# Scaling token tiles before a plain transpose and folding the pre-norm weights into the rounding, in the opening of a hybrid attention block on one core

## The chip, the cores and the metric

The kernel runs on one core of one Trainium2 chip. The metric is the device time of that core in microseconds (us). Engines are named as the profile names them: PE is the matrix engine (its weight loads are listed as PEld), DVE the vector engine, ACT the scalar engine, POOL the general-purpose engine; SP only issues transfers here.

## The reference

One decoder layer on x of 512 tokens by 1024 channels, in float32. Only its first lines bear on the change:

```python
def rms_norm(x, g):
    xf = x.astype(jnp.float32)
    y = xf * lax.rsqrt(jnp.mean(xf * xf, axis=-1, keepdims=True) + RMS_EPS)
    return (y * g.astype(jnp.float32)).astype(x.dtype)

def hybrid_layer(x, norm_pre, w_in, pe_k, w1_k, w2_k, pe_v, w1_v, w2_v, w_a, w_b, w_o, norm_post):
    u = rms_norm(x, norm_pre)
    proj = u @ w_in            # 1024 x 5912: q, k, v, gates, z of two branches, merge gates
    ...                        # compressed, selected and window attention; block attention; gated output projection
    return x + rms_norm(m @ w_o, norm_post)
```

## The kernel before

**What the opening makes.** Every later projection needs u transposed, channels on partitions, and split in two parts: `uh` (u rounded to fp32r) and `ul` (the rest, u − uh), each 128 partitions x 8 channel groups x 512 tokens. A product with a weight split in the same way into hi and lo is three matmuls: hi x uh, hi x ul, lo x uh. The 512 tokens come as four tiles (`tt` = 0 to 3) of 128 tokens x 1024 channels. Per tile the opening computes sums of squares (ACT, `x_stats`), the mean plus epsilon (a small DVE instruction), the power −1/2 on POOL (the result is `rs`), and then transposes in two halves (`h`), four 128x128 transposes each, into a PSUM tile `ut`.

**Tiles 0 and 1 and tiles 2 and 3 differ.** For tiles 0 and 1 (`x_diag`) DVE builds diag(rs), and PE multiplies the x tile with it, which transposes and scales in one matmul (L588). For tiles 2 and 3 ACT first scales x by rs (`x_scale`, L579) and PE then transposes against the identity (L590). In both cases `x_hi` follows for each half: one DVE multiply by the pre-norm weights `npreT` (128x512, L596), one ACT rounding to `uh` (128x512, L600), and `x_low` subtracts on DVE or POOL (128x512, L604).

**The first product, `a_mm`.** For each token tile, 24 matmuls (L626; parts 0, 1, 2 are hi x uh, hi x ul, lo x uh, 8 channel groups each) of 128 tokens by 280 columns of `w_in` go into one PSUM tile `pa`. These 280 columns (`ra`) arrive in four transfers and are split by `wa_hi` (ACT or POOL) and `wa_lo` (DVE or POOL), two channel groups at a time. PSUM tiles `pa` have the tag "s", which has two buffers: tile 2 takes the buffer of tile 0, and tile 3 that of tile 1. `a_evac_act(tt)` (L636, L637) and `a_evac_dve(tt)` (L642) read `pa` out; the DVE part is the last reader.

**What sets the order.** The opening stands in `with tc.manual_schedule()`: each engine runs its own instructions in the order in which the calls are written there, and waits for another engine only where data or a buffer demand it. After it the long stream of projections begins with `mm_kcvc` (L171, L172, L173, 512 tokens at a time), whose weights are split by the pieces `first[0]` to `first[6]`. Thirteen matmuls on zeros (`keep_warm`) run on PE while x is on its way. The transfers are issued on SP: two halves of tile 0, `npre` (the pre-norm weights), tile 1, `ra`, tiles 2 and 3. `klos` and `rowsel` are tiles of a later stage that POOL fills with constants.

Of the kernel before, what the change touches and what calls it, by code (L numbers as in the profile page):

```python
# [41 lines left out]
def hybrid_block(ctx, tc, x, norm_pre, w_in, pe_k, w1_k, w2_k, pe_v, w1_v, w2_v,  # L42
# [509 lines left out]
    rs, up, sss = {}, {}, {}  # L552

    def x_stats(tt, parts=1):
        sq = s4.tile([128, D], F32, tag="s4", name=f"sq_{tt}")
# [5 lines left out]
        sss[tt] = ss  # L561
        if parts == 2:
            r = rs[tt]
            dve.tensor_scalar(ss[:, 0:1], ss[:, 0:1], 1.0 / D, EPS, op0=ALU.mult, op1=ALU.add)
            dve.scalar_tensor_tensor(r, ss[:, 1:2], 1.0 / D, ss[:, 0:1], op0=ALU.mult, op1=ALU.add)
            pool.tensor_tensor(r, r, neghalf, op=ALU.pow)

    def x_stats_r(tt):
        rstd_of(sss[tt][:, 0:1], rs[tt], EPS)

    diag = {}

    def x_diag(tt):
        diag[tt] = early.tile([128, 128], F32, name=f"diag_{tt}")
        dve.tensor_scalar(diag[tt], ident, rs[tt], None, op0=ALU.mult)

    def x_scale(tt, h):
# [74 lines left out]
    with tc.manual_schedule():  # L652
        keep_warm(13)
        x_stats(0, 2)
        pt = ps("t", "npreT_ps")
# [2 lines left out]
        x_diag(0)
        x_transpose(0, 0)
        x_stats_r(1)  # L660
        dve.tensor_copy(npreT, pt[:, 0:KT])
# [480 lines left out]
```

## Time and profile before

| what | value |
|---|---|
| time, median of 3 runs | 471.25 us (471.22 to 471.26) |
| profiled execution, its own time | 471.45 us |
| its span in the profile | 469.7 us, so 1.75 us lie around it |
| PE busy | 459.0 us, 98% of the span |
| DVE, ACT, POOL busy | 326.4, 255.8, 125.8 us |
| first `mm_kcvc` matmul | 26.97 us from the start of the span |

All starts are in us from the start of the span. A row with "x8" is a group of eight instructions that follow one another; the time beside it is from the first one's start to the last one's end. Instructions of one engine overlap, so the distance from start to start is shorter than a duration.

### The profile page before, as it was taken

To read this page: it belongs to the slowest core of one execution; us is meant where nothing else is said; L and a number is where in the kernel's file an instruction comes from. 1 tells how busy PE (TensorE), PEld (TensorE's weight loads), DVE (VectorE), ACT (ScalarE), POOL (GpSimd) and SP (SyncE) were. 2 spreads that over 40 slices of the span, in tenths; PEclk is the share of its full clock that TensorE was granted. 3 is DMA by queue.
4 is the path that set the end of the run, shared out by engine and by line. 5 is a ranking of instruction groups with operands and counts; after the bars stand their busy time and mean duration, and the time that the engine had idled before them with its cause. 6 is when DMAs were issued, how large, how long until landed. Compare 5 with 4: busy or idle time off the path is not lost.

```text
span 469.7 us, 6991 instructions
## 1 busy us (share of the span) xinstructions
PE 459.0 (98%) x2408; PEld 388.1 (83%) x2408; DVE 326.4 (69%) x837; ACT 255.8 (54%) x684; POOL 125.8 (27%) x144
## 2 busy tenths in 40 slices
PE   7999999999999999999999999999999999999994
PEld 6988887888999888788888888887888888888884
DVE  3858868998777878877798978777674264265044
ACT  5754657776566758656675866675433333234021
POOL 6600006433231333323144443432221010020000
...
GB/s 275 191 161 199 45 51 174 2 77 104 7 84 91 1 91 46 45 89 15 77 91 14 76 89 54 38 92 71 64 93 138 109 63 137 89 89 135 45 134 136
DMA packets 45091, 42.08 MB, mean 90 GB/s; under 512 B 1624, under 2 KB 39808, under 8 KB 45056
## 3 DMA queue, kind: packets, MB, share of 16 engines
...
q10 hardware_dynamic: 144, 0.52, 0.3%
...
q14 instruction: 16, 0.13, 0.1%
...
## 4 chain that ended last, share of the span: by engine, by line
PE 88%; DVE 6%; ACT 3%; POOL 1%; issue 1%; POOLq 0%; DVEq 0%; ACTq 0%
PE t L976 5%; PE mm_ga L171 3%; PE mm_ga L172 3%; PE mm_ga L173 3%; PE mm_gb L172 3%; PE mm_gb L173 3%; PE mm_gb L171 3%; PE s L937 3%; PE s L938 3%; PE o L997 3%; PE o L996 3%; PE pa L626 2%; PE mm_qkb L172 2%; PE mm_qkb L173 2%; PE mm_qkb L171 2%; PE mm_vb L290 2%
## 5 line engine op out<-in xcount | busy, mean ns | idle before, releaser
L943 ACT ACTIVATE p<-p,st 128x512 f32<-128x512 f32 (+3 forms) x96 | 53.1, 555 | 23.5 <-DVE st L941 23.2
L955 POOL TENSOR_SCALAR p<-p,st 128x256 f32<-128x256 f32 (+1 forms) x48 | 44.1, 929 | 64.6 <-DVE st L952 22.9
L977 ACT ACTIVATE pt<-t 128x512 fp32r<-128x512 f32 (+1 forms) x72 | 35.4, 524 | 27.4 <-PE t L976 26.8
L978 DVE TENSOR_TENSOR pt<-t,pt 128x512 fp32r<-128x512 f32 (+1 forms) x72 | 40.8, 594 | 8.1 <-ACT pt L977 7.7
L941 DVE CUSTOM_DVE_ANT_0 p<-s,bias_a 128x512 f32<-128x512 f32 (+3 forms) x64 | 29.1, 484 | 10.5 <-PE s L938 10.4
L976 PE MATMUL t<-ident,p 128*128 128x128 f32 x240 | 34.7, 274 | 1.3 <-DVE pt L978 1.0
L976 PEld LDWEIGHTS t<-ident,p 128*128 128x128 f32 x240 | 27.5, 140 | 6.1 <-DVE pt L978 3.3
L354 POOL TENSOR_TENSOR ga<-ga,gb 128x512 f32<-128x512 f32 x8 | 11.7, 1464 | 77.2 <-DVE gb L353 77.2
L1004 POOL TENSOR_TENSOR z<-ot,z 64x512 f32<-64x512 f32 x16 | 20.6, 1285 | 21.8 <-DVE ot L1003 21.8
L171 PE MATMUL mm_qkb<-uh,ws_qkb 128*128 128x512 f32 x64 | 25.8, 404 | 0.0
L171 PE MATMUL mm_gb<-uh,ws_gb 128*128 128x512 f32 x64 | 25.6, 400 | 0.0
L171 PE MATMUL mm_ga<-uh,ws_ga 128*128 128x512 f32 x64 | 25.6, 400 | 0.0
L955 DVE TENSOR_SCALAR p<-p,st 128x512 f32<-128x512 f32 (+1 forms) x48 | 25.2, 564 | 0.5
L172 PE MATMUL mm_gb<-ul,ws_gb 128*128 128x512 f32 x64 | 25.4, 396 | 0.0
L173 PE MATMUL mm_gb<-uh,ws_gb 128*128 128x512 f32 x64 | 25.3, 396 | 0.0
L172 PE MATMUL mm_qkb<-ul,ws_qkb 128*128 128x512 f32 x64 | 25.3, 395 | 0.0
L172 PE MATMUL mm_ga<-ul,ws_ga 128*128 128x512 f32 x64 | 25.3, 395 | 0.0
L173 PE MATMUL mm_ga<-uh,ws_ga 128*128 128x512 f32 x64 | 25.3, 395 | 0.0
L173 PE MATMUL mm_qkb<-uh,ws_qkb 128*128 128x512 f32 x64 | 25.2, 394 | 0.0
L119 DVE TENSOR_TENSOR ws_ab<-raw_ab,ws_ab 128x256 fp32r<-128x256 f32 x32 | 12.8, 455 | 16.7 <-ACT ws_ab L118 16.7
L895 POOL TENSOR_SCALAR bias_a<-dbase 128x512 f32<-128x512 f32 x8 | 13.2, 1650 | 37.8 <-DVE st L941 33.0
L895 POOL TENSOR_SCALAR bias_b<-dbase 128x512 f32<-128x512 f32 x8 | 12.3, 1543 | 38.2 <-DVE st L941 38.2
...
## 6 DMA issues: line engine op xcount, KB each, us to landing
...
```

Of the source, the lines that this page charges most:

```text
L171: mm(dst, v[:, 0, k], rh(n), start=(n == 0), stop=False)
L172: mm(dst, v[:, 0, k], rl(n), start=False, stop=False)
L173: mm(dst, v[:, 1, k], rh(n), start=False, stop=(n == len(kts) - 1))
L895: pool.tensor_scalar(t, dbase, slope, None, op0=ALU.mult)
L937: mm(sp[:, 0:nn], q, hi, start=True, stop=False)
L941: dve.tensor_tensor_reduce(pp, src, bias[:, 384 - 128 * i:512], 1.0, 3.0e38, ALU.add, ALU.min, st[:, 0, i:i + 1])
L943: act.activation(pp, pp, AF.Exp, bias=st[:, 0, i:i + 1], scale=-1.0, accum_out=st[:, 1, i:i + 1])
L955: (dve if i >= 2 else pool).tensor_scalar(pp, pp, st[:, 1, i:i + 1], None, op0=ALU.mult)
L976: pe_eng.transpose(tp[:, b * 128:(b + 1) * 128], p_of(u, i)[:, 128 * j:128 * j + 128], ident)
L977: act.activation(h[:, c0:c0 + n], tp[:, 0:n], AF.Copy)
L978: dve.tensor_tensor(l[:, c0:c0 + n], tp[:, 0:n], f(h[:, c0:c0 + n]), op=ALU.subtract)
L1004: pool.tensor_tensor(zs[zt][mine], t[mine], zs[zt][mine], op=ALU.mult)
```

## The change

In its parts:

1. `npre` is fetched as the first transfer on ACT's queue, no longer on SP between tiles 0 and 1, and its transpose `npreT` is made earlier, with the last two of the thirteen warm-up matmuls behind it.
2. The constant fills of `klos` and `rowsel`, which POOL ran before its first power, move into `clear()`, called after `first[6]`.
3. All four tiles are scaled on DVE (`x_scale`, one `tensor_scalar` of 128x512 per half) and then transposed against the identity. `diag` and ACT's scaling are gone.
4. The multiply by `npreT` is gone as an instruction. `x_hi` is four ACT instructions of 128x128 per half, which read PSUM and scale by a column of `npreT` while they round; `x_low` is four DVE instructions of 128x128 per half, (ut x npreT) − uh. All `x_low` stand on DVE now, and POOL's share of `wa_lo` too; POOL takes two of the four `wa_hi`.
5. The opening has a new order, with `a_mm` in smaller pieces (channel groups 0 to 3 and 4 to 7 apart).

```diff
+    npre = early.tile([KT, 128], F32, name="npre")
+    nc.scalar.dma_start(npre, norm_pre.rearrange("(k p) -> k p", k=KT))
...
     load_x(0, 2)
-    nc.sync.dma_start(npre, norm_pre.rearrange("(k p) -> k p", k=KT))
     load_x(1)
...
+    def x_scale(tt, h, eng=None):
         c = slice(512 * h, 512 * h + 512)
-        act.activation(xt[tt][:, c], xt[tt][:, c], AF.Copy, scale=rs[tt])
+        if eng is None:
+            dve.tensor_scalar(xt[tt][:, c], xt[tt][:, c], rs[tt], None, op0=ALU.mult)
...
     def x_transpose(tt, h):
-
         pt = ps("to"[h], f"ut_{tt}_{h}")
         for k in range(4):
             kk = 4 * h + k
-            o, i = pt[:, k * 128:(k + 1) * 128], xt[tt][:, kk * 128:(kk + 1) * 128]
-            if tt in diag:
-                mm(o, i, diag[tt], start=True, stop=True)
-            else:
-                pe_eng.transpose(o, i, ident)
-        up[tt, h] = pt
+            pe_eng.transpose(pt[:, k * 128:(k + 1) * 128], xt[tt][:, kk * 128:(kk + 1) * 128], ident)
+        ut[tt, h] = pt
 
     def x_hi(tt, h):
-
-        u = xt[tt][:, 512 * h:512 * h + 512].rearrange("p (k t) -> p k t", k=4)
-        dve.tensor_tensor(u, up[tt, h].rearrange("p (k t) -> p k t", k=4),
-                          npreT[:, 4 * h:4 * h + 4, None].to_broadcast([128, 4, 128]), op=ALU.mult)
-        hi = uh[:, 4 * h:4 * h + 4, tt * 128:tt * 128 + 128]
-        up[tt, h] = (u, hi)
-        act.activation(hi, u, AF.Copy)
-
-    def x_low(tt, h, eng=dve):
-        u, hi = up[tt, h]
-        eng.tensor_tensor(ul[:, 4 * h:4 * h + 4, tt * 128:tt * 128 + 128], u, f(hi), op=ALU.subtract)
+        for k in range(4):
+            kk = 4 * h + k
+            act.activation(uh[:, kk, tt * 128:tt * 128 + 128], ut[tt, h][:, k * 128:(k + 1) * 128], AF.Copy,
+                           scale=npreT[:, kk:kk + 1])
+
+    def x_low(tt, h):
+        for k in range(4):
+            kk = 4 * h + k
+            a = slice(tt * 128, tt * 128 + 128)
+            dve.scalar_tensor_tensor(ul[:, kk, a], ut[tt, h][:, k * 128:(k + 1) * 128], npreT[:, kk:kk + 1],
+                                     f(uh[:, kk, a]), op0=ALU.mult, op1=ALU.subtract)
...
         x_low(2, 0)
+        a_evac_act(0)
+        x_scale(3, 0)
+        a_mm(2, (0,), 2, lo)
+        x_scale(3, 1)
+        x_low(2, 1)
+        a_mm(2, (0,), 2, hi)
+        a_evac_act(1)
+        x_transpose(3, 0)
         x_transpose(3, 1)
         a_evac_dve(0)
-        a_mm(1, (1,), 1)
+        a_mm(2, (2,), 1)
...
-        a_mm(3, (0, 1, 2))
+        a_mm(3, (0, 2, 1), 1)
         first[6]()
+        clear()
```

What stands where is told by each engine's own order. First DVE, from the statistics of tile 2 on (`rs_196`, now `rs_239`) to the read-out of `pa` of tile 0 (L642, now L638, which writes `v_slc` and `v_win`), before:

```order
13 L514 TENSOR_SCALAR rs_196<-ss_195 128x1
14 L613 TENSOR_TENSOR wa_hl<-ra,wa_hl 128x560 x2
15 L514 TENSOR_SCALAR rs_226<-ss_225 128x1
16 L613 TENSOR_TENSOR wa_hl<-ra,wa_hl 128x560
17 L604 TENSOR_TENSOR ul<-x_96,uh 128x4x128
18 L596 TENSOR_TENSOR x_97<-ut_0_250,npreT 128x512
19 L596 TENSOR_TENSOR x_97<-ut_1_264,npreT 128x512
20 L604 TENSOR_TENSOR ul<-x_97,uh 128x4x128
21 L642 TENSOR_TENSOR v_slc<-pa_198,v_slc 128x2x64
22 L642 TENSOR_TENSOR v_win<-pa_198,v_win 128x2x64
```

and now (`x_98`, `x_99`, `x_100` are the token tiles 1, 2, 3; `ut_0_184` and `ut_1_190` belong to tile 1, `ut_0_273` and `ut_1_278` to tile 2):

```order
11 L561 TENSOR_SCALAR rs_239<-ss_238 128x1
12 L589 SCALAR_TENSOR_TENSOR ul<-ut_0_184,npreT,uh 128x128 x4
13 L589 SCALAR_TENSOR_TENSOR ul<-ut_1_190,npreT,uh 128x128 x4
14 L567 TENSOR_SCALAR x_99<-x_99,rs_239 128x512 x2
15 L561 TENSOR_SCALAR rs_285<-ss_284 128x1
16 L599 TENSOR_TENSOR wa_hl<-ra,wa_hl 128x560 x2
17 L589 SCALAR_TENSOR_TENSOR ul<-ut_0_273,npreT,uh 128x128 x4
18 L567 TENSOR_SCALAR x_100<-x_100,rs_285 128x512 x2
19 L589 SCALAR_TENSOR_TENSOR ul<-ut_1_278,npreT,uh 128x128 x4
20 L638 TENSOR_TENSOR v_slc<-pa_199,v_slc 128x2x64
21 L638 TENSOR_TENSOR v_win<-pa_199,v_win 128x2x64
```

Between the statistics of tile 2 and the read-out of tile 0 DVE had seven large instructions and one small; now it has 6 of 128x512 or 128x560, 16 of 128x128 and one small, with the scaling of tile 3 and all of tile 2's `x_low` ahead of the read-out. The second place is ACT, from the first rounding on, before (L610 is `wa_hi`, L600 `x_hi`):

```order
5 L610 ACTIVATE wa_hl<-ra 128x560 x2
6 L600 ACTIVATE uh<-x_95 128x4x128
7 L610 ACTIVATE wa_hl<-ra 128x560
8 L600 ACTIVATE uh<-x_95 128x4x128
9 L560 ACTIVATE sq_194,ss_195<-x_97 128x1024
10 L600 ACTIVATE uh<-x_96 128x4x128 x2
11 L560 ACTIVATE sq_224,ss_225<-x_98 128x1024
12 L579 ACTIVATE x_97<-x_97,rs_196 128x512 x2
13 L579 ACTIVATE x_98<-x_98,rs_226 128x512 x2
```

and now (L582 is `x_hi`, L596 `wa_hi`, L556 the squares of tiles 2 and 3):

```order
6 L582 ACTIVATE uh<-ut_0_156,npreT 128x128 x4
7 L582 ACTIVATE uh<-ut_1_162,npreT 128x128 x4
8 L596 ACTIVATE wa_hl<-ra 128x560
9 L582 ACTIVATE uh<-ut_0_184,npreT 128x128 x4
10 L582 ACTIVATE uh<-ut_1_190,npreT 128x128 x4
11 L596 ACTIVATE wa_hl<-ra 128x560
12 L556 ACTIVATE sq_237,ss_238<-x_99 128x1024
13 L556 ACTIVATE sq_283,ss_284<-x_100 128x1024
```

The squares of tile 2 stood behind three `wa_hi` and two roundings, and stand now behind two `wa_hi` and sixteen small roundings. The third place is PE, around the first product of tile 2 (`pa_311`, now `pa_316`), before (`x_97` and `x_98` are tiles 2 and 3 there, `pa_228` is tile 1):

```order
12 L590 MATMUL ut_0_250<-ident,x_97 128x128 x4
13 L626 MATMUL pa_198<-wa_hl,uh 128x280 x4
14 L590 MATMUL ut_1_264<-ident,x_97 128x128 x4
15 L626 MATMUL pa_228<-wa_hl,uh 128x280 x4
16 L590 MATMUL ut_1_279<-ident,x_98 128x128 x4
17 L590 MATMUL ut_0_288<-ident,x_98 128x128 x4
18 L626 MATMUL pa_228<-wa_hl,ul 128x280 x8
19 L626 MATMUL pa_311<-wa_hl,uh 128x280 x16
20 L626 MATMUL pa_311<-wa_hl,ul 128x280 x8
```

and now (`pa_199`, `pa_221`, `pa_316`, `pa_398` are the products of tiles 0 to 3):

```order
17 L575 MATMUL ut_0_273<-ident,x_99 128x128 x4
18 L575 MATMUL ut_1_278<-ident,x_99 128x128 x4
19 L622 MATMUL pa_199<-wa_hl,uh 128x280 x4
20 L622 MATMUL pa_221<-wa_hl,uh 128x280 x4
21 L622 MATMUL pa_316<-wa_hl,uh 128x280 x8
22 L575 MATMUL ut_0_334<-ident,x_100 128x128 x4
23 L575 MATMUL ut_1_339<-ident,x_100 128x128 x4
24 L622 MATMUL pa_316<-wa_hl,uh 128x280 x8
25 L622 MATMUL pa_316<-wa_hl,ul 128x280 x8
26 L753 MATMUL ps_pe_k<-ident,cv_k 128x16
27 L171 MATMUL mm_kcvc_470<-uh,ws_kcvc_380 128x512
28 L753 MATMUL ps_pe_v<-ident,cv_v 128x16
```

The transposes of tile 3 stood ahead of the first matmul into `pa` of tile 2, with a whole part of tile 1 between them and it; now eight matmuls into `pa` of tile 2 stand ahead of them. The product of tile 3, 24 matmuls, stands now behind the first two matmuls of `mm_kcvc` (L171, L172) and ahead of the third (L173). Behind that L173 the order of every engine is the one of before but for names.

## Rows read from the trace of the kernel before

**Rows 1.** The page: the span, and the engines' busy time, share of the span and instructions.

```profile
span 469.7 us, 6991 instructions
PE 459.0 (98%) x2408; PEld 388.1 (83%) x2408; DVE 326.4 (69%) x837; ACT 255.8 (54%) x684; POOL 125.8 (27%) x144
```

**Rows 2.** Windows of the opening: stretch and its length, busy us (and instructions) of each engine, granted PE clock, share of the DMA engines, GB/s.

```profile
5.00:10.00 5.00, 4.13 (x31) 3.55 (x30) 2.06 (x7) 2.29 (x4) 2.32 (x5) 1.00 1.06 321
10.00:15.00 5.00, 4.17 (x31) 3.56 (x29) 4.80 (x8) 4.19 (x9) 2.99 (x3) 1.00 1.06 368
15.00:20.00 5.00, 5.00 (x41) 4.94 (x42) 4.23 (x9) 4.93 (x11) 3.52 (x6) 1.00 0.89 220
20.00:25.00 5.00, 5.00 (x41) 5.00 (x41) 3.90 (x11) 3.14 (x13) 1.99 (x4) 1.00 0.00 0
```

**Rows 3.** The chain of work that ended last, its opening in order of time: start us, us, what.

```profile
5.82 0.52 POOL klos L752
6.34 0.53 POOL rs L566
6.89 0.30 DVE diag L575
7.24 2.96 PE ut L588 x24
10.22 0.69 DVE x L596
10.91 2.74 DVE ul L604 x2
13.69 3.09 PE pa L626 x20
...
19.61 7.21 PE pa L626 x56
27.04 0.43 PE mm_kcvc L171
```

**Rows 4.** Timeline of the statistics of tiles 0 and 1: start us, us, engine, line, operation, out and in, count, and in brackets the idle time before it and its releaser.

```profile
4.85 0.16 DVE L565 SCALAR_TENSOR_TENSOR rs<-ss 128x1 f32<-128x1 f32 x1 [0.49 <-ACT sq L560]
6.46 1.06 ACT L560 ACTIVATE sq<-x 128x1024 f32<-128x1024 f32 x1 [1.64 <-DMA x<-in_x_dram]
7.42 0.19 ACT L560 ACTIVATION_READ_ACCUMULATOR sq<-x 128x1 f32 x1
7.88 0.55 POOL L515 TENSOR_TENSOR rs<-rs,neghalf 128x1 f32<-128x1 f32 x1 [1.02 <-DVE npreT L661]
14.38 0.98 POOL L515 TENSOR_TENSOR rs<-rs,neghalf 128x1 f32<-128x1 f32 x1 [1.29 <-DVE rs L514]
```

**Rows 5.** Timeline of PE, the same columns: transposes against diag, plain transposes, the first product, and the first rows of `mm_kcvc`.

```profile
7.24 3.84 PE L588 MATMUL ut<-diag,x 128*128 128x128 f32 x32 [0.87 <-DVE diag L575]
18.58 1.03 PE L590 MATMUL ut<-ident,x 128*128 128x128 f32 x8
20.48 2.22 PE L626 MATMUL pa<-wa_hl,uh 128*128 128x280 f32 x16
26.75 0.23 PE L758 MATMUL ps_pe_k<-ident,cv_k 16*128 16x16 f32 x1
26.97 0.51 PE L171 MATMUL mm_kcvc<-uh,ws_kcvc 128*128 128x512 f32 x1
27.32 0.40 PE L172 MATMUL mm_kcvc<-ul,ws_kcvc 128*128 128x512 f32 x1
27.55 0.39 PE L173 MATMUL mm_kcvc<-uh,ws_kcvc 128*128 128x512 f32 x1
```

**Rows 6.** ACT: timeline rows of L579 (128x512 from SBUF, scaled by a column), L600 (128x512 from SBUF, no column) and L636 (128x128 from PSUM, no column), and by source line the one place with 128x128 from PSUM scaled by a column (L811; durations min/median/max in ns).

```profile
15.85 2.73 ACT L579 ACTIVATE x<-x,rs 128x512 f32<-128x512 f32 x4
20.92 1.17 ACT L600 ACTIVATE uh<-x 128x512 fp32r<-128x512 f32 x2 [0.89 <-DVE x L596]
19.01 0.25 ACT L636 ACTIVATE v_slc<-pa 128x128 fp32r<-128x128 f32 x1
19.16 0.26 ACT L636 ACTIVATE v_win<-pa 128x128 fp32r<-128x128 f32 x1
L811 ACT ACTIVATE vcs<-pk_v,rowsel x2: 367/367/367, 82.2 to 83.4; 128x128 fp32r<-128x128 f32 x2
```

**Rows 7.** DVE: timeline rows of L642 (128x128, PSUM and SBUF), of L613 (`wa_lo`) and L596 (128x512), by source line the one place with a 128x128 product with a column and a second operand (L812), and the group of 128x512 products with a column (L955: count, busy us, mean ns).

```profile
19.74 0.28 DVE L642 TENSOR_TENSOR v_slc<-pa,v_slc 128x128 fp32r<-128x128 f32 x1
19.94 0.28 DVE L642 TENSOR_TENSOR v_win<-pa,v_win 128x128 fp32r<-128x128 f32 x1
14.22 1.38 DVE L613 TENSOR_TENSOR wa_hl<-ra,wa_hl 128x560 fp32r<-128x560 f32 x2
20.14 1.28 DVE L596 TENSOR_TENSOR x<-ut,npreT 128x512 f32<-128x512 f32 x2
L812 DVE SCALAR_TENSOR_TENSOR vcs<-pk_v,rowsel,vcs x2: 341/343/345, 83.1 to 84.3; 128x128 fp32r<-128x128 f32 x2
L955 DVE TENSOR_SCALAR p<-p,st 128x512 f32<-128x512 f32 x24 | 12.7, 529 | 0.5
```

**Rows 8.** Windows at the end of the span, columns as in rows 2, and from the timeline of PE the warm-up matmuls (as a whole, and two pieces of it).

```profile
463.00:465.00 2.00, 0.61 (x6) 0.41 (x4) 0.49 (x2) 0.47 (x2) 0.48 (x1) 1.00 0.19 72
465.00:465.50 0.50, 0.00 (x0) 0.00 (x0) 0.40 (x1) 0.00 (x0) 0.07 (x1) 1.00 0.00 0
465.50:466.00 0.50, 0.00 (x0) 0.00 (x0) 0.50 (x2) 0.00 (x0) 0.00 (x0) 0.54 0.00 0
...
1.44 4.78 PE L650 MATMUL warmup<-warmup 128*128 128x512 f32 x13 [1.44 <-DVE warmup L83]
2.03 1.05 PE L650 MATMUL warmup<-warmup 128*128 128x512 f32 x2
4.90 0.62 PE L650 MATMUL warmup<-warmup 128*128 128x512 f32 x2
```

More of the change, by code (lines that the diff above doesn't have):

```diff
@@ L560, in x_stats @@
             act.activation(sq[:, n * w:n * w + w], xt[tt][:, n * w:n * w + w], AF.Square, accum_out=ss[:, n:n + 1])
-        sss[tt] = ss
+        part = EPS
         if parts == 2:
[L563 to L577, printed above, removed]
+            part = ss[:, 0:1]
+            dve.tensor_scalar(part, part, 1.0 / D, EPS, op0=ALU.mult, op1=ALU.add)
+        dve.tensor_scalar(r, ss[:, parts - 1:parts], 1.0 / D, part, op0=ALU.mult, op1=ALU.add)
+        pool.tensor_tensor(r, r, neghalf, op=ALU.pow)
+    def x_scale(tt, h, eng=None):
         c = slice(512 * h, 512 * h + 512)
-        act.activation(xt[tt][:, c], xt[tt][:, c], AF.Copy, scale=rs[tt])
+        if eng is None:
+            dve.tensor_scalar(xt[tt][:, c], xt[tt][:, c], rs[tt], None, op0=ALU.mult)
+        else:
+            act.activation(xt[tt][:, c], xt[tt][:, c], AF.Copy, scale=rs[tt])
     def x_transpose(tt, h):
@@ L613, in wa_lo, with clear @@
         eng.tensor_tensor(wa_hl[:, 1, k:k + 2], ra[:, k:k + 2], f(wa_hl[:, 0, k:k + 2]), op=ALU.subtract)
+    def clear():
+        pool.memset(rowsel, 0.0)
+        for i in range(4):
+            pool.memset(rowsel[32 * i:32 * i + 32, i % 2:i % 2 + 1], 1.0)
+        for t in klos:
+            for n in range(2):
+                pool.memset(f(t[64:128, n, 0]), 0.0)
+                pool.memset(f(t[0:64, n, 1]), 0.0)
     vst["slc"], vst["win"] = s4tile("v_slc"), s4tile("v_win")
@@ L656, in hybrid_block @@
         pe_eng.transpose(pt[:, 0:KT], npre, ident[0:KT, 0:KT])
+        dve.tensor_copy(npreT, pt[:, 0:KT])
+        keep_warm(2)
+        lo, hi = range(0, 4), range(4, 8)
+        x_scale(0, 0)
+        x_transpose(0, 0)
+        x_scale(0, 1)
+        x_transpose(0, 1)
         x_stats(1)
[L658 to L661, printed above, removed]
+        x_hi(0, 0)
+        x_hi(0, 1)
+        x_scale(1, 0)
+        wa_hi(2, pool)
         wa_hi(0)
-        x_transpose(0, 1)
@@ L664, in hybrid_block @@
-        x_diag(1)
         x_transpose(1, 0)
-        wa_hi(2)
-        x_hi(0, 0)
+        x_scale(1, 1)
+        x_transpose(1, 1)
+        x_low(0, 0)
+        a_mm(0, (0,), 2, lo)
+        x_hi(1, 0)
+        x_low(0, 1)
+        a_mm(0, (1,), 2, lo)
         wa_hi(4, pool)
+        x_hi(1, 1)
+        a_mm(1, (0,), 2, lo)
         wa_hi(6)
-        wa_lo(4, pool)
-        x_transpose(1, 1)
-        x_hi(0, 1)
+        wa_lo(0)
+        wa_lo(2)
+        a_mm(0, (0, 1), 2, hi)
         x_stats(2)
-        a_mm(0, (0,))
@@ L675, in hybrid_block @@
-        x_hi(1, 0)
-        x_low(0, 0)
-        x_low(0, 1)
-        x_hi(1, 1)
-        x_stats_r(2)
-        a_mm(0, (1,))
-        wa_lo(0)
-        x_stats(3)
-        a_mm(1, (0,))
-        a_mm(0, (2,), 2, (4, 5, 0, 1))
-        x_scale(2, 0)
-        x_scale(2, 1)
-        wa_lo(2)
-        x_stats_r(3)
-        a_mm(1, (2,), 2, (4, 5, 0, 1))
-        x_transpose(2, 0)
-        wa_lo(6)
-        x_scale(3, 1)
-        a_mm(0, (2,), 2, (2, 3, 6, 7))
-        x_low(1, 1, pool)
-        x_low(1, 0)
@@ L696, in hybrid_block @@
-        x_scale(3, 0)
-        x_transpose(2, 1)
-        x_hi(2, 0)
-        a_evac_act(0)
-        a_mm(1, (2,), 1, (2, 3, 6, 7))
+        x_low(1, 0)
+        a_mm(1, (0,), 2, hi)
+        x_low(1, 1)
+        a_mm(0, (2,), 2, lo)
+        a_mm(1, (2,), 2, lo)
+        x_scale(2, 0)
+        a_mm(1, (1,), 2, lo)
+        x_scale(2, 1)
+        a_mm(1, (1,), 2, hi)
+        x_transpose(2, 0)
+        x_transpose(2, 1)
+        x_stats(3)
+        wa_lo(4)
+        x_hi(2, 0)
+        wa_lo(6)
@@ L701, in hybrid_block @@
+        x_hi(2, 1)
+        a_mm(0, (2,), 2, hi)
+        a_mm(1, (2,), 2, hi)
+        x_low(2, 0)
+        a_evac_act(0)
+        x_scale(3, 0)
+        a_mm(2, (0,), 2, lo)
+        x_scale(3, 1)
+        x_low(2, 1)
+        a_mm(2, (0,), 2, hi)
+        a_evac_act(1)
+        x_transpose(3, 0)
         x_transpose(3, 1)
-        x_hi(2, 1)
-        x_low(2, 0)
-        x_low(2, 1, pool)
-        x_transpose(3, 0)
         a_evac_dve(0)
-        a_mm(1, (1,), 1)
+        a_mm(2, (2,), 1)
         x_hi(3, 0)
@@ L709, in hybrid_block @@
         x_hi(3, 1)
-        a_evac_act(1)
-        a_mm(2, (0,))
         x_low(3, 0)
-        a_mm(2, (2,), 1)
         a_mm(2, (1,), 1)
@@ L745, in hybrid_block @@
     vcs = const.tile([128, 2, 2, 128], F32R, name="vcs")
-    pool.memset(rowsel, 0.0)
-    for i in range(4):
-        pool.memset(rowsel[32 * i:32 * i + 32, i % 2:i % 2 + 1], 1.0)
-    for t in klos:
-        for n in range(2):
-            pool.memset(f(t[64:128, n, 0]), 0.0)
-            pool.memset(f(t[0:64, n, 1]), 0.0)
     blk, pe2, w2t = {}, {}, {}
```

10 lines of the change are left out of this document (3 added, 7 removed).

## The prediction

> **What bounds the kernel now.** The page comes first: PE is busy for 459.0 of 469.7 us [rows 1], so whatever is late in the opening is late at the end, as long as the stream behind it is the same and PE has its work ready. The windows say where PE is not full: 0.87 us are missing between 5 and 10 us and 0.83 us between 10 and 15; from 15 us on every stretch is full [rows 2]. The chain says what those two gaps wait for: POOL's fills up to 6.34 us, then the power of tile 0 and diag; later the rounding of tile 0 and the two slow `x_low` of DVE (2.74 us) up to 13.69 [rows 3]. From there it is PE itself to the first `mm_kcvc`. So I take one number as the yardstick, the start of the first L173, 27.55 us [rows 5]: behind it the order of all engines is unchanged, and a shift there is a shift of the end. What the change can gain is bounded: the two gaps, and cheaper PE work.
>
> **Prices, from start to start.** PE: 32 matmuls against diag take 3.84 us, 0.23 for each transpose (it leaves two records); 8 plain ones take 1.03 us, 0.109 each; an `a_mm` 0.129 [rows 5]. Sixteen cheaper transposes save 1.8 us of PE time. ACT: L636 (128x128, PSUM, no column) lasts 0.25 us and starts 0.15 apart, so two neighbours overlap by about 0.11. A column as scale costs about 0.11 more from start to start: four L579 in 2.73 us are 0.67 apart, two L600 in 1.17 us 0.56. L811, which is the new `x_hi` in shape, source and column, lasts 0.367, so I take 0.26 [rows 6]. The bounds are 0.15 (the column is free) and 0.37 (no overlap). DVE: L642 lasts 0.28 and starts 0.20 apart, an overlap of 0.08. L812, which is the new `x_low`, lasts 0.343, so 0.26, with bounds 0.20 and 0.34. The new scaling is like L955 at 128x512: 0.529, so 0.45; `wa_lo` 0.65, the read-out 0.20 [rows 7]. `wa_hi` on ACT keeps about 0.57 and the square 1.05, with its read 1.15 until the statistic can start. For half a tile that makes ACT 1.04 where one rounding took 0.56 (tiles 0 and 1), and DVE 0.45 + 1.04 where multiply and subtraction took 0.60 + 0.60: both engines get more work, of the kind that the next stage waits for.
>
> Beside the rows: the Trainium skill, "VectorE: DVE Perf Modes", section "The TRN2 errata — SBUF-src ops pay a fixed extra latency per instruction", speaks against the split into pieces of 128: a fixed cost is paid per instruction, and it advises tiles of 512 elements or more. The trace bears it out: 0.28 us for the 128 columns of L642, about 0.68 for the 512 of L596 [rows 7]. The Trainium skill, "ScalarE: Activation LUTs", section "What ACT_TABLE_LOAD costs", gives 186 ns plus 0.833 ns a column, some 93 ns for a column operand and 93 ns of overlap: as an estimate from that page 0.29 us for each `x_hi`, where the rows gave 0.26; by it the first L173 would come about 0.9 us later than in my sum.
>
> **The change, followed in time.** *Start.* The fills leave the front of POOL, so the first power starts when the statistic is there, at 4.85 + 0.16 = 5.01 instead of 6.34 [rows 3, 4], and ends at 5.6. Two scalings and the first transposes follow; all eight of tile 0 are done at 7.5. Before, 16 of the 32 records of L588 were through at about 9.1 [rows 5]. So 1.6 us are won here. The fills cost nothing where they go: behind the gates of tile 2 (about 27 us), some 4.5 us on a POOL that has little to do, for tiles of a later stage. *Tile 1's x* lies one small transfer earlier in SP's queue; the bounds are nothing and 0.4 us earlier. I take nothing, because the square of tile 1 would then only reach ACT's list sooner, and that list is what follows.
>
> *ACT.* The square of tile 1 ends at 7.6 as before [rows 4]. Then eight `x_hi` of tile 0 at 0.26 (9.7), a `wa_hi` (10.3), eight `x_hi` of tile 1 (12.35; their transposes end at 10.05), the second `wa_hi` (12.9), the square of tile 2 with its read (14.0). Before, the statistic of tile 2 had its square ready at 12.9: it is 1.1 us later. PE has the hi halves only with that second `wa_hi`, so it waits until 12.95, where `a_mm` ran from 10.83 on with two gaps of 0.35 and 0.48.
>
> *DVE.* It waits for the square of tile 2, idle from 12.8, because `rs_239` stands ahead of `x_low` of tile 1. From 14.0: statistic 0.07, eight `x_low` 2.08 (16.15), two scalings of tile 2 0.90 (17.05; its power, 0.98 on POOL beside a busy DVE [rows 4], is done by 15.1), statistic 0.07, two `wa_lo` 1.30 (18.5), four `x_low` 1.04 (19.55), two scalings of tile 3 0.90 (20.5), four `x_low` 1.04 (21.5), two read-outs 0.20 + 0.28 (22.0).
>
> *PE.* It has worked off what it was allowed by 19.5 us: all of tiles 0 and 1 and the transposes of tile 2. The next matmul writes `pa` of tile 2 into the buffer of tile 0, which DVE lets go at 22.0. So PE waits about 2.5 us, from 19.5 to 22.05, and tile 3's transposes are queued behind the waiting matmul and can't fill the gap; before, they had run at 18.58 and the read-out was done at 20.2, before anyone asked for the buffer. From 22.05: 8 `a_mm` 1.03, 8 transposes 0.87, 16 `a_mm` 2.06 (26.0); the small L758, L171 and L172 with the pitches of rows 5 0.8 (26.8); the 24 `a_mm` of tile 3, now inside `mm_kcvc`, 3.1. The first L173 starts at 29.9: 27.55 + 2.35. As a balance: −1.8 of PE work, −0.8 of the earlier beginning, +4.9 of more waiting. The same list, made for the order of before with the same prices, gives 27.49 for its 27.55, so the method is good to some tenths; the prices of the 64 small instructions are what it hangs on. In that list L173 shifts by 0.28 us for each hundredth of a us more on every `x_hi` and by 0.16 for each on every `x_low`.
>
> **The clock on top.** At the end of the span PE's last matmul ends at 463.6, and 1.9 us later the granted clock falls from 1.00 to 0.5, the lower of its two levels, 1.2 GHz [rows 8]. The new wait is 2.5 us. So the clock can fall in it, and the matmuls behind it start at half speed. What that costs is bounded by the warm-up: its matmuls stood 0.42 us apart at 2.03 and 0.23 at 4.9 (the durations 0.63 and 0.39 taken off), 4.78 us for what takes 3.2 at full pace, a loss of 1.6 us [rows 8]; the clock column reads 1.00 there, so that the clock was low is my reading of the spacing. Such a loss here is hidden where PE waits again and not hidden where it bounds, which it does from 22.05 on, so I take most of it, 1.0 to 1.5. An earlier fall in the thin stretch from 6 to 13 us would be covered for the most part by the wait until 12.95.
>
> **The sum.** Against the profiled execution: 471.45 + 2.35 = 473.8 without a fall, which is 473.6 against the median of 471.25 (the execution lies 0.2 above it). With the fall 1.0 to 1.5 more, 474.5 to 475.1.
>
> **The rivals.** What this measurement can't tell from no change is about 0.2%, 0.94 us.
> (1) The wait of 2.5 us comes, the clock falls: 474.5 to 475.1. For it: the 1.9 us at the end. Against it: that is a single fall, and the 0.87 us wait of the opening left no trace in the clock column. Chance 0.48.
> (2) The wait comes, the clock stays at 1.00: 473.0 to 474.0, around 473.6. Chance 0.29.
> (3) The columns are free, 0.15 and 0.20 us for the small instructions. ACT's list is then 1.8 us shorter by 12.9 and DVE's about 1 us shorter; the read-out ends near 19.7 and L173 comes at 27.5 to 27.7: no change, 471.2. Against it stand L811 and L812 with 0.367 and 0.343, measured in the same shape. Halves of it (only ACT, only DVE) give 28.6 and 29.0. Chance 0.13.
> (4) The other side: small instructions in a run overlap down to what their 128 columns take. From 128x512 to 128x128 the durations of rows 6 and 7 fall by about 0.36 and 0.40 us for 384 columns, so 128 columns are 0.12 on ACT and 0.14 on DVE. Then both lists end before PE needs them, the 1.8 us of cheaper transposes come through up to the data's arrival, and L173 starts at 25.7 to 26.7: 469.4 to 470.4. It decides below about 0.14 (ACT) and 0.17 (DVE). For it: nothing in the trace has a run of more than two such instructions, so the overlap in a long run isn't seen. Against it: L636 and L642, without a column, already take 0.15 and 0.20. Chance 0.10.
>
> **The numbers.** Likeliest is (1), at its lower end 474.5. The range from 471.2 to 475.6 takes in (1) but for its upper tail, (2) and the middle of (3), and leaves out (4), about 0.17 in all; by (1) alone it would be 474.0 to 475.6, and the bound with no overlap at all (L173 at 34.2) lies beyond. Faster by over 0.2%: (4), 0.09. Within: (3) and the edge of (2) and (4), 0.14. Slower: 0.77.
>
> **What would show it.** Right: the first power at about 5.1; ACT's `x_hi` 0.26 apart and DVE's `x_low` too; the statistic of tile 2 at 14.0; a wait of PE of 2 to 3 us before the first `a_mm` of tile 2, released by DVE's read-out of tile 0 (L638); the first L173 near 29.9; the granted clock at 0.5 behind that wait. Wrong: small instructions nearer than 0.17 apart, PE full from 15 us on, or a stream behind L173 that doesn't keep the shift because it had waits of its own.

## The result and the profile after

The changed kernel takes 476.38 us (median of 4 runs, 476.05 to 477.86) against 471.24 for the kernel before: a ratio of 1.0116, 95% interval 1.0097 to 1.0135, so 5.1 us slower. Forecast were 474.5 us and a range of 471.2 to 475.6. The direction and the mechanism were right, the size was too small, and the time lies 0.8 us above the range.

The profiled execution took 476.15 us with a span of 474.3. Its page (the lines that answer to [rows 1]):

```profile
span 474.3 us, 6997 instructions
PE 459.7 (97%) x2392; PEld 387.7 (82%) x2392; DVE 328.3 (69%) x862; ACT 256.6 (54%) x703; POOL 122.7 (26%) x142
```

PE is busy for 0.7 us more than before; the span is 4.6 us longer, so the time went into waiting, and into matmuls that take longer. The timeline of PE (columns as in [rows 4]) says where:

```profile
6.62 1.09 PE L575 MATMUL ut<-ident,x 128*128 128x128 f32 x8
9.95 1.09 PE L575 MATMUL ut<-ident,x 128*128 128x128 f32 x8 [2.24 <-DVE x L567]
...
13.48 0.52 PE L622 MATMUL pa<-wa_hl,uh 128*128 128x280 f32 x2 [0.56 <-ACT wa_hl L596]
...
18.28 1.70 PE L622 MATMUL pa<-wa_hl,uh 128*128 128x280 f32 x8
22.54 2.20 PE L622 MATMUL pa<-wa_hl,uh 128*128 128x280 f32 x8 [2.56 <-DVE v_win L638]
...
29.04 2.22 PE L622 MATMUL pa<-wa_hl,uh 128*128 128x280 f32 x16
31.10 1.19 PE L622 MATMUL pa<-wa_hl,ul 128*128 128x280 f32 x8
32.13 0.39 PE L173 MATMUL mm_kcvc<-uh,ws_kcvc 128*128 128x512 f32 x1
```

The first L173 starts at 32.13 instead of 27.55 [rows 5], 4.58 us later, which is the longer span: from there to the end it is 442.1 us in both kernels. The row at 22.54 is the wait that was forecast: 2.56 us for DVE's read-out of tile 0 (`v_win`, L638), at the first `a_mm` of tile 2. Eight such matmuls take 2.20 us there, and 1.19 us in the row at 31.10. The windows around the wait show why (columns as in [rows 2]; the granted clock stands just ahead of the DMA share):

```profile
20.00:21.00 1.00, 0.00 (x0) 0.00 (x0) 1.00 (x4) 0.87 (x7) 0.45 (x2) 1.00 0.02 8
...
21.50:22.00 0.50, 0.00 (x0) 0.00 (x0) 0.50 (x3) 0.00 (x0) 0.12 (x1) 0.93 0.07 16
22.00:22.50 0.50, 0.00 (x0) 0.00 (x0) 0.39 (x2) 0.00 (x0) 0.00 (x0) 0.50 0.00 0
...
25.00:25.50 0.50, 0.50 (x5) 0.50 (x4) 0.00 (x0) 0.00 (x0) 0.00 (x0) 0.65 0.00 0
25.50:26.00 0.50, 0.50 (x7) 0.50 (x6) 0.00 (x0) 0.42 (x2) 0.00 (x0) 1.00 0.00 0
```

PE stood still from 20.0; the granted clock fell to 0.50, the lower level of 1.2 GHz, just before 22, about 2 us into the wait, and rose again at about 25.35 (the 0.65 is the mean of its half microsecond), when PE had worked for some 2.8 us. What filled ACT and DVE until then is in their timelines, ACT's first:

```profile
7.04 1.06 ACT L556 ACTIVATE sq<-x 128x1024 f32<-128x1024 f32 x1 [2.21 <-DMA x<-in_x_dram]
8.10 2.15 ACT L582 ACTIVATE uh<-ut,npreT 128x128 fp32r<-128x128 f32 x8
10.65 2.22 ACT L582 ACTIVATE uh<-ut,npreT 128x128 fp32r<-128x128 f32 x8
```

and DVE's:

```profile
14.50 0.15 DVE L561 TENSOR_SCALAR rs<-ss 128x1 f32<-128x1 f32 x1 [0.83 <-ACT sq L556]
14.57 2.16 DVE L589 SCALAR_TENSOR_TENSOR ul<-ut,npreT,uh 128x128 fp32r<-128x128 f32 x8
...
22.11 0.28 DVE L638 TENSOR_TENSOR v_win<-pa,v_win 128x128 fp32r<-128x128 f32 x1
```

Eight small roundings take 2.15 us and eight small subtractions 2.16, from start to start 0.25 us on ACT and 0.26 on DVE; the prediction had 0.26 for both. One row differs from [rows 4]: the square of tile 1 starts at 7.04, not at 6.46, because tile 1 landed at 7.02. From there everything on ACT and DVE is 0.3 to 0.5 us behind the predicted list; the statistic of tile 2, for one, comes at 14.50 instead of 14.0.

### The profile page after: what moved, and what is told of

Same layout as the page of the kernel before. It is cut to its first block, busy times and chain, and to the rows that moved or that the text cites. A ratio compares the mean times of both kernels' runs of the same rounds, so it can differ in the third digit from the quotient of the medians.

```text
span 474.3 us, 6997 instructions
## 1 busy us (share of the span) xinstructions
PE 459.7 (97%) x2392; PEld 387.7 (82%) x2392; DVE 328.3 (69%) x862; ACT 256.6 (54%) x703; POOL 122.7 (26%) x142
## 4 chain that ended last, share of the span: by engine, by line
PE 86%; DVE 5%; SPq 3%; ACT 3%; issue 1%; DMA 0%; POOLq 0%; DVEq 0%; ACTq 0%
PE t L971 5%; PE mm_ga L173 3%; PE mm_ga L172 3%; PE mm_ga L171 3%; PE mm_gb L172 3%; PE mm_gb L173 3%; PE s L932 3%; PE mm_gb L171 3%; PE s L933 3%; PE o L992 3%; PE o L991 3%; PE mm_qkb L171 2%; PE mm_qkb L173 2%; PE mm_qkb L172 2%; PE mm_vb L290 2%; PE mm_vb L291 2%
## 5 line engine op out<-in xcount | busy, mean ns | idle before, releaser
L171 PE MATMUL mm_qkb<-uh,ws_qkb 128*128 128x512 f32 x64 | 25.9, 404 | 0.0
L171 PE MATMUL mm_gb<-uh,ws_gb 128*128 128x512 f32 x64 | 25.6, 400 | 0.0
L171 PE MATMUL mm_ga<-uh,ws_ga 128*128 128x512 f32 x64 | 25.5, 399 | 0.0
L172 PE MATMUL mm_gb<-ul,ws_gb 128*128 128x512 f32 x64 | 25.4, 396 | 0.0
L173 PE MATMUL mm_gb<-uh,ws_gb 128*128 128x512 f32 x64 | 25.3, 396 | 0.0
L173 PE MATMUL mm_ga<-uh,ws_ga 128*128 128x512 f32 x64 | 25.3, 395 | 0.0
L172 PE MATMUL mm_ga<-ul,ws_ga 128*128 128x512 f32 x64 | 25.3, 395 | 0.0
L172 PE MATMUL mm_qkb<-ul,ws_qkb 128*128 128x512 f32 x64 | 25.2, 395 | 0.0
L173 PE MATMUL mm_qkb<-uh,ws_qkb 128*128 128x512 f32 x64 | 25.2, 395 | 0.0
```

Of the source, the lines that this page charges most:

```text
L171: mm(dst, v[:, 0, k], rh(n), start=(n == 0), stop=False)
L172: mm(dst, v[:, 0, k], rl(n), start=False, stop=False)
L173: mm(dst, v[:, 1, k], rh(n), start=False, stop=(n == len(kts) - 1))
```

## The experiments

Times are medians of three or five rounds against the kernel before on the same chip (471.17 to 471.22 there).

**1. The read-out ahead of tile 3's scaling.**

```diff
         a_evac_act(0)
+        a_evac_dve(0)
         x_scale(3, 0)
...
         x_transpose(3, 1)
-        a_evac_dve(0)
```

> The changed kernel with one move: DVE's read-out of tile 0 (a_evac_dve(0)) stands right behind ACT's and ahead of the scaling of tile 3. Theory (the time went to the wait for the PSUM buffer of tile 0 and to the clock that falls in it): the buffer is free at about 20.7 us instead of 22.4, PE waits 0.6 to 0.8 us instead of 2.56, the granted clock stays at 1.00, and the first L173 starts at 29.0 (32.13 less 1.85 less 1.24), some 3.1 us less than the changed kernel: 472.8 to 473.3. Rival (the longer lists of small instructions on ACT and DVE are the cost wherever PE meets them): the same wait comes back a few instructions later, before the transposes of tile 3 or the ul part of tile 2, and L173 stays at 31.5 or later, 475.5 and above.

Measured: 473.60 us, ratio 1.0052 (1.0035 to 1.0069), 2.8 us less than the changed kernel. Timeline of PE:

```profile
21.10 1.29 PE L622 MATMUL pa<-wa_hl,uh 128*128 128x280 f32 x8 [1.14 <-DVE v_win L638]
...
29.41 0.39 PE L173 MATMUL mm_kcvc<-uh,ws_kcvc 128*128 128x512 f32 x1
```

The wait shrank from 2.56 to 1.14 us, the matmuls behind it run at full pace, and no new wait took its place. The wait is longer than expected because DVE's read-out itself waited 0.32 us for ACT's. So more than half of the loss hangs on where one pair of small DVE instructions stood.

**2. The wait kept, but filled.**

```diff
+        keep_warm(10)
         a_mm(2, (0,), 2, lo)
```

> The changed kernel with ten more warm-up matmuls on zeros on PE ahead of the first a_mm of tile 2, so that the wait is there but PE is busy in it. Theory (1.2 us of the loss are matmuls at the lower clock behind the wait): the buffer is still released at 22.4, the granted clock stays at 1.00, the eight a_mm behind the wait stand 0.129 apart instead of 0.233, L173 starts at 30.9 and the time is 475.1, and the runs of the kernel lie closer together than 476.05 to 477.86. Rival (the clock is a bystander, what follows the wait is bound by DVE or ACT): L173 stays at 32.1 and the time at 476.1 to 476.4.

Measured: 474.71 us, ratio 1.0076 (1.0061 to 1.0091), 1.7 us less than the changed kernel, though PE does ten more matmuls. Not all of it is the clock: in the profiled execution tile 1 landed at 6.18, and the buffer was released at 21.83 instead of 22.39. Windows and timeline of PE:

```profile
20.00:21.00 1.00, 1.00 (x6) 0.82 (x5) 1.00 (x5) 0.31 (x3) 1.00 (x3) 1.00 0.05 16
22.00:23.00 1.00, 1.00 (x8) 1.00 (x9) 0.00 (x0) 0.00 (x0) 0.00 (x0) 1.00 0.00 0
```

```profile
19.25 2.48 PE L646 MATMUL warmup<-warmup 128*128 128x512 f32 x10
21.98 1.28 PE L622 MATMUL pa<-wa_hl,uh 128*128 128x280 f32 x8 [0.25 <-DVE v_win L638]
...
30.29 0.39 PE L173 MATMUL mm_kcvc<-uh,ws_kcvc 128*128 128x512 f32 x1
```

The clock stays at 1.00. From the first matmul behind the wait to the first L173 it is 8.31 us here and 9.59 in the changed kernel (32.13 less 22.54): the lower clock cost 1.28 us in that execution. That the runs would lie closer together did not come out clearly: 474.13 to 475.51 against 476.05 to 477.86.

**3. npre back on SP.**

```diff
-    nc.scalar.dma_start(npre, norm_pre.rearrange("(k p) -> k p", k=KT))
...
     load_x(0, 2)
+    nc.sync.dma_start(npre, norm_pre.rearrange("(k p) -> k p", k=KT))
     load_x(1)
```

> The changed kernel with the fetch of npre back on SP between tile 0 and tile 1. Theory (the fetch of npre on ACT's queue, or SP's transfers without it in between, makes tile 1 land at 7.02 instead of 6.44, and ACT's whole list runs 0.5 us late behind it): tile 1 lands at 6.4 to 6.5, the square of tile 2 and the release of the PSUM buffer come 0.5 us earlier, the wait of PE ends at 22.0, L173 at 31.6: about 475.8. Rival (the landing varies by itself or depends on something else, such as the fills that left POOL): tile 1 lands at 7.0 again and nothing moves.

Measured: 475.87 us, ratio 1.0097 (1.0082 to 1.0112): not to be told from the changed kernel. Tile 1 landed at 6.50, as expected, but the release of the buffer did not come earlier (22.55, against 22.39): the copy of npreT, which stands ahead of the first scaling on DVE, now came at 6.74 and took the place of tile 1. The windows around the wait are the more telling part:

```profile
21.00:22.00 1.00, 0.00 (x0) 0.00 (x0) 1.00 (x5) 0.03 (x1) 0.78 (x3) 1.00 0.06 16
22.00:22.70 0.70, 0.01 (x1) 0.04 (x1) 0.55 (x3) 0.00 (x0) 0.00 (x0) 1.00 0.00 0
22.70:24.00 1.30, 1.30 (x10) 1.30 (x11) 0.00 (x0) 0.00 (x0) 0.00 (x0) 1.00 0.07 13
```

and in the timeline of PE:

```profile
22.70 1.28 PE L622 MATMUL pa<-wa_hl,uh 128*128 128x280 f32 x8 [2.56 <-DVE v_win L638]
31.01 0.39 PE L173 MATMUL mm_kcvc<-uh,ws_kcvc 128*128 128x512 f32 x1
```

The wait of PE is 2.56 us, the same as in the changed kernel, and the clock did not fall in it; the first L173 starts at 31.01, 8.31 us behind the wait, as in experiment 2. So whether the clock falls in a wait of this length differs from one execution to the next. The four executions of this experiment are of both kinds: two have a mean granted clock of 0.999 and a span of 473.1 us, two 0.992 and 0.993 and 474.5 us.

**4. The kernel before with the fills late.** The memsets of `klos` and `rowsel` move into `clear()` behind `first[6]()`, as in the changed kernel, and nothing else.

> The kernel before with one part of the change: the fills of klos and rowsel stand behind first[6] and not ahead of the first power. Theory (ACT's list from the landing of tile 1 and the transfers of ra set the pace behind tile 0): the first power starts at 5.1 and the transposes of tile 0 at 5.9 instead of 7.24, but PE then waits for tile 1 and ra, and L173 moves by 0 to 0.4 us earlier, 470.8 to 471.3. Rival (the fills were the head of the whole chain): 1.2 to 1.3 us come through, 470.0.

Measured: 471.14 us against 471.17, ratio 0.9999 (0.9990 to 1.0008): no change. The first power starts at 5.10 instead of 6.31, and PE then waits for tile 1 and for DVE instead:

```profile
6.20 2.05 PE L588 MATMUL ut<-diag,x 128*128 128x128 f32 x16
8.74 2.05 PE L588 MATMUL ut<-diag,x 128*128 128x128 f32 x16 [0.49 <-DVE diag L575]
...
13.19 0.79 PE L635 MATMUL pa<-wa_hl,ul 128*128 128x280 f32 x4 [0.49 <-DVE ul L604]
```

The first L173 starts at 27.06 in this execution, 0.49 us earlier than in [rows 5]. But its time, 470.89, lies 0.25 below its median, and that of the kernel before 0.2 above: the start of L173 is that of one execution, and executions of one kernel lie 0.5 us and more apart.

**5. A third buffer for tile 2.**

```diff
-            apt[tt] = ps("s", f"pa_{tt}")
+            apt[tt] = ps("mm" if tt == 2 else "s", f"pa_{tt}")
```

> The changed kernel with one line altered: the product of tile 2 takes a PSUM buffer of another tag, so that nothing on PE waits for DVE's read-out of tile 0. Order and instructions on ACT and DVE are those of the changed kernel. Theory (this wait and the clock behind it are the loss, the longer lists are not yet): no wait over 0.5 us on PE after 15 us, clock at 1.00, first L173 at 27.2 to 28.1, so within 0.2% of the kernel before, 470.9 to 471.9. Rival (the lists of small instructions hold PE up at the next place: transposes of tile 3 behind the scaling, ul part of tile 2, or the first mm_kcvc): PE waits there for 1 us or more and the time is 472.7 or above.

Measured: 471.76 us, ratio 1.0012 (1.0003 to 1.0021). One line takes away 4.6 of the 5.1 us; PE has no wait behind 12 us. What is left is 0.6 us. Two things in the profiled execution bear on it: tile 1 landed at 6.90, and the windows and PE's timeline show a fall of the clock:

```profile
8.00:10.00 2.00, 0.16 (x1) 0.16 (x2) 1.22 (x3) 2.00 (x10) 1.17 (x2) 1.00 1.13 353
11.00:12.00 1.00, 1.00 (x7) 1.00 (x7) 1.00 (x5) 1.00 (x5) 0.28 (x1) 0.62 1.03 383
13.00:14.00 1.00, 1.00 (x6) 1.00 (x5) 0.55 (x1) 1.00 (x2) 0.00 (x0) 0.50 1.10 348
15.00:20.00 5.00, 5.00 (x40) 4.78 (x40) 4.42 (x15) 2.22 (x10) 2.22 (x3) 1.00 0.82 204
27.90 0.39 PE L173 MATMUL mm_kcvc<-uh,ws_kcvc 128*128 128x512 f32 x1
```

The clock fell at about 11.2, behind the thin stretch between the transposes of tile 0 and the first product, and the first L173 starts at 27.90. Experiments 7 and 9 say which of the two weighs more.

**6 and 7. npreT early, alone and with the buffer.** The transpose of npre stands behind five warm-up matmuls and its copy right behind it.

```diff
-        keep_warm(11)
-        x_stats(0, 2)
+        keep_warm(5)
         pt = ps("t", "npreT_ps")
         pe_eng.transpose(pt[:, 0:KT], npre, ident[0:KT, 0:KT])
         dve.tensor_copy(npreT, pt[:, 0:KT])
-        keep_warm(2)
+        keep_warm(6)
+        x_stats(0, 2)
```

> The changed kernel with the transpose of npre behind five warm-up matmuls instead of eleven, and its copy on DVE accordingly early. Theory (in the executions in which the warm-up runs longer at the low pace, the copy of npreT on DVE, and with it the first scaling, waits for PE; ACT's list then starts 0.5 us late even where tile 1 lands early): the first scaling starts right behind the power, at 5.6 to 5.9 us, ACT's first x_hi follows the square of tile 1 without a gap; the time goes down by 0.2 to 0.6 us against the changed kernel, to 475.8 to 476.2. Rival (only the landing of tile 1 sets the head of ACT's list): no change, 476.4.

> Both of these alterations together. Theory: the gains add up, L173 at 26.8 to 27.7, 470.4 to 471.5, at most 0.15% faster than the kernel before. Rival (with the wait gone PE works off its queue, and what the head of ACT's list wins is lost at the second wa_hi or the second wa_lo): the same as with the buffer alone.

Measured: 476.47 us alone (ratio 1.0107, 1.0087 to 1.0128) and 472.11 with the buffer (1.0014, 1.0005 to 1.0023). Neither differs from its partner without the early transpose. In the profiled executions tile 1 landed at 6.79 and 7.41, and its square, not npreT, was the head of ACT's list. In experiment 6 the second half of tile 0 landed late as well (5.02), so the first scaling came at 6.75 and not at 5.6 to 5.9. Both rivals held. The windows of experiment 7 show the clock at 1.00 throughout the opening, and yet its first L173 comes later than that of experiment 5:

```profile
28.18 0.39 PE L173 MATMUL mm_kcvc<-uh,ws_kcvc 128*128 128x512 f32 x1
```

**8. A version with the weights spread out as a row.** `npre` as one row times a row of ones on PE, copied to a tile `npreB`; one instruction of 512 columns each for scaling, rounding and subtraction; the third buffer; a new order. Its core:

```diff
-            dve.tensor_scalar(xt[tt][:, c], xt[tt][:, c], rs[tt], None, op0=ALU.mult)
+            dve.scalar_tensor_tensor(xt[tt][:, c], xt[tt][:, c], rs[tt], npreB[:, c], op0=ALU.mult, op1=ALU.mult)
...
+        mm(pt, ones, npre[:, 512 * h:512 * h + 512], start=True, stop=True)
```

> A version meant to beat both: the pre-norm weights are spread over all partitions at the start (an outer product with ones on PE, two copies to SBUF) and multiplied in with rs before the transpose, in one DVE instruction of 128x512; x_hi is one ACT rounding of 128x512 from PSUM and x_low one DVE subtraction of 128x512. The product of tile 2 takes the third buffer, the fills stay late, and the order of the opening is new, with tile 3's transposes ahead of the product of tile 2. If the split into pieces of 128 columns is what made the lists long (0.26 us a piece on both engines, 1.04 for half a tile, where one piece of 512 takes 0.56 on ACT and 0.60 on DVE), PE is full from about 11 us on and L173 comes at 25.2 to 26.3, 1.2 to 2.2 us before that of the kernel before: 469.0 to 470.1. If transfers or PE itself bound the opening, it stays at 470.9 to 471.4.

Measured: 472.78 us, ratio 1.0033 (1.0022 to 1.0044), slower than the kernel before. PE was full from 14 us on, where about 11 were expected. The opening was late:

```profile
3.02 3.78 PE L595 MATMUL npre_ps<-npre,ones 1*128 1x512 f32 x4
6.72 2.08 PE L652 MATMUL warmup<-warmup 128*128 128x512 f32 x4
...
28.83 0.40 PE L173 MATMUL mm_kcvc<-uh,ws_kcvc 128*128 128x512 f32 x1
```

The two row products took 3.78 us on PE (each leaves two records, 1.1 us long), and the warm-up matmuls behind them, still 0.43 us apart, held PE until 8.60, when the transposes of tile 0 started; in the changed kernel they started at 6.62. Part of the delay may be chance: the second half of tile 0 landed at 4.83 (4.09 in the changed kernel), and the first scaling, at 6.95, waited for the power that hangs on it. The version says nothing against the wide instructions; its own start was priced too low.

**9. Small fetch as a spacer on SP.** Experiment 7 with a second fetch of npre, into a tile that nobody reads, where npre stood on SP.

```diff
     load_x(0, 2)
+    nc.sync.dma_start(spacer, norm_pre.rearrange("(k p) -> k p", k=KT))
     load_x(1)
```

> The changed kernel with the third buffer and the early transpose of npre, and with a second small fetch (4 KB into a tile that nobody reads) on SP where npre stood, so that tile 1 and ra are issued as in the kernel before while npre stays on ACT's queue. Theory (tile 1 lands late and scattered because SP issues it 0.4 us sooner, so that its packets share the DMA engines with tile 0 and ra; in the runs so far 6.2 to 7.4 with npre on ACT's queue, 6.4 to 6.5 with it on SP): tile 1 lands at 6.4 to 6.6, ACT's list starts 0.3 to 0.8 us earlier, L173 at 27.2 to 27.6, 471.0 to 471.5. Rival (the landing depends on npre being on ACT's queue, or is chance): 6.8 or later and 472.1 as without the spacer.

Measured: 471.49 us against 471.22, ratio 1.0004 (0.9995 to 1.0013); tile 1 landed at 6.37. Timelines of ACT, and then of PE:

```profile
6.39 1.06 ACT L558 ACTIVATE sq<-x 128x1024 f32<-128x1024 f32 x1 [1.50 <-DMA x<-in_x_dram]
27.09 0.39 PE L173 MATMUL mm_kcvc<-uh,ws_kcvc 128*128 128x512 f32 x1
```

With the third buffer, the early npreT and the spacer the changed kernel is as fast as the one before. Against experiment 7, also without a fall in the opening, tile 1 landed 1.04 us earlier and L173 starts 1.09 earlier: in these two traces, with the buffer's wait gone, the landing comes through to L173. Experiment 5, with its landing at 6.90, lies about 0.25 us above a straight line between these two, an estimate from three single traces of what its fall of the clock cost.

**10. The kernel before with npre on ACT's queue,** and nothing else changed.

> The kernel before with npre on ACT's queue as its only change. Theory: tile 1 lands between 6.6 and 7.2 instead of 6.4, its statistics, diag and transposes come as much later, and as PE has little else then, 0.2 to 0.6 us of it reach the first L173 (27.8 to 28.1): 471.4 to 471.8. Rival: tile 1 lands at 6.4 or sooner and the time stays at 471.2 or falls.

Measured: 471.54 us against 471.22, ratio 1.0006 (0.9997 to 1.0015); tile 1 landed at 6.70. The time is where it was expected, but the interval takes in no change, and the trace does not bear the theory out: its first L173 starts at 27.41, where 27.8 to 28.1 were expected and the kernel before has 27.55.

**11. The kernel before, POOL relieved.** Late fills, third buffer, and the `wa_lo(4)` and the `x_low(1, 1)` that POOL ran stand on DVE.

```diff
-        wa_lo(4, pool)
...
         a_mm(0, (1,))
+        wa_lo(4)
         wa_lo(0)
...
-        x_low(1, 1, pool)
+        x_low(1, 1)
         x_low(1, 0)
```

> The kernel before with the late fills, the third buffer for the product of tile 2, and the two instructions that POOL ran beside a busy DVE between 11 and 18.6 us (one wa_lo, one x_low) on DVE. The roundings and subtractions stay 512 columns wide, the transposes of tiles 0 and 1 stay those against diag. If the slow pair of x_low (2.74 us where two take 1.3) came from POOL's work beside it, the pair takes 1.3 us, the wait of PE of 0.48 at 13.7 is gone and L173 comes 0.4 to 1.0 us earlier: 470.2 to 470.8. If DVE's two more instructions or the rounding of tile 1 hold PE up instead, 471.0 to 471.5.

Measured: 470.26 us against 471.22, ratio 0.9983 (0.9974 to 0.9992). This one is faster than both kernels, by about 0.2% against the one before. In its timeline of DVE the slow pair is nearly gone, though tile 1 landed late (6.93) in that execution; the kernel before, with POOL's instruction beside the pair, stands below it:

```profile
11.10 1.55 DVE L604 TENSOR_TENSOR ul<-x,uh 128x512 fp32r<-128x512 f32 x2
10.83 2.81 DVE L604 TENSOR_TENSOR ul<-x,uh 128x512 fp32r<-128x512 f32 x2
11.37 1.71 POOL L613 TENSOR_TENSOR wa_hl<-ra,wa_hl 128x560 fp32r<-128x560 f32 x1
```

The late fills alone don't do it (2.59 us in experiment 4). How much of the gain in time is due to the pair and how much to the buffer was not taken apart. The profiled execution does not show the gain: it took 470.97 us, one of the slower ones, and its first L173 starts at 27.07, as in experiment 4.

## Why the direction was right and the size was not

**The mechanism held.** The added wait stands at the instruction that was named, behind the releaser that was named, 2.56 us long where 2.5 were forecast. Experiment 5 takes away only the buffer's dependence and with it 4.6 of 5.1 us, without touching ACT's or DVE's work; experiment 1 gets 2.8 of them by order alone.

**The prices held.** In runs of eight the small instructions stand 0.25 us apart on ACT and 0.26 on DVE, where 0.26 had been taken from the lone pairs of [rows 6, 7]. So rival (3), which needed 0.15 and 0.20, and rival (4), which needed less than 0.14 and 0.17, fell at their first condition. The Trainium skill, "ScalarE: Activation LUTs", section "What ACT_TABLE_LOAD costs", gives by the estimate made there 0.29 us for `x_hi`. The trace has 0.25 (durations of 0.35 to 0.46, a mean of 0.39 us), and the measurement decides.

**The clock held, as a chance.** It fell in the changed kernel's profiled execution and cost 1.28 us, inside the 1.0 to 1.5 of the sum. In experiment 3 the same wait passed without a fall. Which kind an execution was shows in its mean granted clock and its span. In experiments 3 and 6, nearly the same program, three executions have 0.999 and a span of 473.1 us; their other five, and all four of the changed kernel, have 0.996 or less and spans of 474.1 to 475.9. So rivals (1) and (2) are two kinds of executions rather than two theories, and the four of the changed kernel all look like kind (1). The slowest, 477.86 us, has the lowest clock, 0.989; it was not profiled, and where its clock was low stays open. At the end of the span, the ground on which the prediction stood, the time to the fall differs too: 1.9 us behind PE's last matmul in the kernel before, 4.3 in the changed one (468.2 to 472.5). Experiment 5 shows a fall in the thin stretch of the beginning; the prediction had put it aside as covered for the most part, and the estimate of 0.25 us at experiment 9 agrees.

**The balance.** The first L173 was forecast at 29.9 with full clock and 30.9 to 31.4 with the fall; it came at 32.13. Of the 4.58 us of shift, 2.35 are the shift forecast for full clock and 1.28 the clock. The step that failed is not the wait but the size of two terms ahead of it and behind it:

- The landing of tile 1, the head of ACT's list. The prediction took "nothing" for the earlier issue, with the bounds "nothing and 0.4 us earlier", and let the square of tile 1 end "at 7.6 as before". Tile 1 landed 0.58 us later in the profiled execution (7.02 for 6.44), and the release of the buffer came at 22.39 instead of 22.0, with PE's start at 22.54 instead of 22.05: 0.49 us. A bound above zero was missing. In the executions with npre on ACT's queue and no spacer tile 1 landed at 6.18 to 7.41 (eight of them, half at 6.9 or later), in those with a small fetch on SP between tiles 0 and 1 at 6.37 to 6.93 (five). Experiments 9 and 10 point to the place of the small fetch, but their 0.6 and 0.3 us are too near the spread, and the first group also has the two earliest landings: the cause of the late landing is not shown. An early landing alone did not always help, either: where tile 1 landed at 6.30 and 6.50 (experiments 1 and 3), the copy of `npreT`, behind the warm-up matmuls at 6.74, held the same place, and the statistic of tile 2 came at 14.48 and 14.67, as late as here (14.50); with both at 6.2 (experiment 2) it came at 13.94. The prediction's list has no such term.
- The small matmuls among L171 and L172. The prediction gave 0.8 us from the end of tile 2's `a_mm` to the first of tile 3; it is 1.17 (from 26.84 + 8 x 0.129 = 27.87 to 29.04), 0.37 more. The two small L758, now L753, stood side by side before (26.75 and 26.83); now one stands ahead of each of the two large matmuls, as the order printed with the change shows, and L171 is followed 0.43 us later and not 0.35.

The forecast, the clock and these two make 4.49 of the 4.58 us. Around the span lie 1.85 us where they were 1.75, and the profiled execution of the kernel before lay 0.2 us above its median, that of the changed kernel 0.2 below it; no run shows why. The range failed at its upper end: 475.6 leaves 0.5 us above the forecast with the whole cost of the clock (473.6 + 1.5), and the two mis-sized terms come to 0.86. The point, 474.5, took 0.9 for a fall that cost 1.28.

**The cheap parts were cheap.** The fills are worth nothing at the front (experiment 4) and cost nothing behind: in the prediction they were counted as 0.8 us of an earlier beginning, which the wait for tile 1 then ate. The cheaper transposes save their 1.8 us (1.9 by the prediction's own prices, sixteen times 0.23 less 0.109) only where PE is the bound; up to 22 us it is not. The Trainium skill's rule against small pieces ("VectorE: DVE Perf Modes", section "The TRN2 errata — SBUF-src ops pay a fixed extra latency per instruction") is given there for sources in SBUF. The small pieces here read `ut` in PSUM, and the rows agree with it, 1.00 us on ACT and 1.04 on DVE for four pieces where one wide instruction takes 0.56 or 0.60. But experiment 9 shows that the time doesn't follow from it by itself: with the wait for the buffer gone the longer lists cost no more than the rest of the change gives back.
